# Small products of TensorE regrouped in a decoder block: sums, diagonals, transposes, and the first value weights

## The chip, the core and the metric

The kernel runs on one core of a Trainium2 chip. The metric is the device time of one execution in microseconds (us). Each time is the median of several runs. A profiled execution gives, beside its own time, the span from the first to the last instruction on the core's engines: TensorE (PE, with its weight loads as PEld), VectorE (DVE), ScalarE (ACT), GpSimd (POOL) and SyncE (SP, which issues DMAs).

## What is computed

A decoder block for 256 tokens and a width of 1024, in float32. Cut to what matters:

```
h    = rmsnorm(x);  proj = h @ w_in          # latents 384 + 256, 64 rope columns, q k v (8 x 128), gates
y_a  = attention(rope/latent q, k, v) @ w_o_mla   # q, k, v from rmsnorm(latents) @ w_uq, w_ukv
y_b  = attention(rope(q), rope(k), v) @ w_o_moba  # one block of 256 keys, causal
x    = x + (g_a * y_a + g_b * y_b) @ w_out        # g = sigmoid(gates)
h    = rmsnorm(x)
x    = x + (silu(u1) * u2) @ w_down               # u = causal conv of width 3 over h @ w_up
out  = rmsnorm(x)
```

Both attention branches have 8 heads. Each is causal softmax attention over 256 keys. The norms of the latents need the sum of squares over 384 and over 256 features for each token.

## The kernel before

Activations lie in SBUF with features on partitions and tokens along the row, so that most products have 128 x 128 weights as the stationary operand and 256 tokens as the moving one. For the values and the output projection it is the other way: 128 tokens are stationary and 512 weight columns move. Every product is done in three: both operands are split into a high half, rounded to fp32r, and a low half (the rest), and high x high, low x high and high x low are summed in one PSUM bank (`mm3`, L341). `split` (L346) makes the halves: ScalarE copies with rounding, VectorE subtracts.

Weights arrive in units of 2048 columns (1 MB), one DMA each from SyncE, in a fixed order (`PLAN`, L63). Three buffers hold raw units (`raw`), three the high halves (`whi`), three the low halves (`wlo`). `weights` (L353) issues the load of a unit and splits it in two pieces of 1024 columns.

Order of work: eight input tiles and the latents' weights ("first"), the values (four units "v", two for each half of the columns, `proj_tokens`, L463), then for each of four pairs of heads of the MoBA branch q, gate and k units and one call of `attention` (L603), then four calls for the latent branch, the output projections, and the FFN stage with 22 "up" units.

The order of instructions on each engine is not written by hand. `Program` (L144) records all operations with their dependencies; operations recorded inside `P.together()` form one atom that is issued without a break and that depends on all that its parts need. `emit` (L212) then runs a list scheduler: on each engine it takes, among the operations that are ready at the time at which the engine could go on, the one that was recorded first. Times come from a table of prices (`price`, L283): a transpose 0.11 us, a float32 product 4 x 0.107 us, GpSimd's power 0.63 us and its other operations 0.15 us and a little for each element, and fixed delays between engines. SyncE's loads keep their recorded order. On the chip the engines run in the emitted order and wait on semaphores.

The places that the change touches:

- Rows from columns: a factor for each token (such as the inverse root mean square) exists with tokens on partitions and is needed as a row on all partitions. `to_rows` (L439) multiplies the identity by the factor on VectorE (a diagonal, tile `diag`, two buffers) and multiplies a matrix of ones by it on TensorE in plain float32. It is called for the input's factor (L545), for both latents' factors (L581) and for the FFN's factor (L821).
- The sums of squares of the latents are four float32 products with one column of ones (`lat_sums`, L562). They are recorded between the products of the second half of the values (`between`, L474), after the first four of eight groups.
- From the sums, VectorE and GpSimd form the latents' factors (`r_lat`, L572 to L578): for each latent VectorE multiplies, GpSimd scales, raises to -0.5 and multiplies.
- `keep_values` (L551) scales the values out of PSUM and splits them; for the second half it is recorded before the factors (L571).
- In `attention` the normalised exponentials of a head (tile `e`) are transposed by TensorE, three blocks of 128 x 128, split into `ph` and `pl`, and multiplied with the values into a bank `av`; then the second head follows.

PSUM has eight banks: three `mm`, three `sc`, two `av`, each used in turn.

Of the kernel before, what the change touches and what calls it, by code (L numbers as in the profile page):

```python
# [8 lines left out]


# [2 lines left out]

# [1 line left out]

# [13 lines left out]
S = 256  # L29
# [277 lines left out]
def hybrid_block(ctx: ExitStack, tc: tile.TileContext, x, par, con, fnorm, wpack, out):  # L307
# [3 lines left out]
    P = Program(tc.nc)  # L311
    act, dve, pool, pe, sp = P.act, P.dve, P.pool, P.pe, P.sp

    def T(name, shape, dt=F32):
        return sb.tile([128] + shape, dt, tag=name, name=name)
# [14 lines left out]
    sc_bank = Ring("sc", 3, [512], space=ps)  # L330
    av_bank = Ring("av", 2, [512], space=ps)
# [6 lines left out]
    def mm(o, l, r, start, stop, skip=True):  # L338
        pe.matmul(o, lhsT=l, rhs=r, start=start, stop=stop, skip_group_check=skip)
# [6 lines left out]
    def split(hi, lo, src):  # L346
        act.copy(hi, src)
        dve.tensor_sub(lo, src, f32(hi))
# [1 line left out]

    units = iter(range(len(PLAN)))

    def weights(kind, i, *cuts):  # L353

        u = next(units)
        assert PLAN[u] == (kind, i), (PLAN[u], kind, i)
        n = SIZE.get(kind, UNIT)
        raw, hi, lo = raws(), his(), los()
        cuts = cuts or (n // 2, n)
        sp.dma_start(raw[:, :n], wpack[u, :, :n])  # L360
        a = 0
        for b in cuts:
            split(hi[:, a:b], lo[:, a:b], raw[:, a:b])
            a = b
        return hi, lo

    def groups(wv, k, c):
        return [t.rearrange("p (m k c) -> p m k c", k=k, c=c) for t in wv]
# [3 lines left out]
    ident = cst[:, 4 * S : 4 * S + 128]  # L372
# [8 lines left out]
    ones = T("ones", [128])  # L381
    pool.memset(ones, 1.0)
    o = av_bank()
# [7 lines left out]
    xh, xl = T("XH", [KT, S], F32R), T("XL", [KT, S], F32R)  # L391
# [42 lines left out]
        used[0] += n  # L434
        return smalls[:, used[0] - n : used[0]]

    diag = Ring("diag", 2, [128])

    def to_rows(o, col2):  # L439

        for tt in range(2):
            dg = diag()
            dve.tensor_scalar(dg, ident, col2[:, tt : tt + 1], None, op0=ALU.mult)
            mm(o[:, 128 * tt : 128 * tt + 128], ones, dg, True, True, False)

    def feature_tile(o, m, w, ah, al, ks, first, last):
# [13 lines left out]
                                 m == 0 and k == 0, k > 0)  # L460
        return o

    def proj_tokens(kind, i0, o, ah, al, *between):  # L463

        for part in range(2):
            wv = groups(weights(kind, i0 + part), 4, 512)
            for k4 in range(4):
                k = 4 * part + k4
                with P.together():
                    for tt in range(2):  # L470
                        c = slice(128 * tt, 128 * tt + 128)
                        mm3(o[tt], ah[:, k, c], al[:, k, c], wv[0][:, 0, k4], wv[1][:, 0, k4],
                            k == 0, k == KT - 1)
                if k < len(between):  # L474
                    between[k]()

    def two(ap):
        return ap[:, None, :].to_broadcast([ap.shape[0], 2, S])
# [24 lines left out]
    lat, sq = gate[:, 0:6], gate[:, 6:11]  # L503
# [7 lines left out]
    for j in range(KT // 2):  # L511
        wv = first_unit(j)
        for kk in range(2):
            k = 2 * j + kk
# [25 lines left out]
    rsqrt(r1, ss[:, 0:2], D, 2)  # L540
    pool.tensor_tensor(r1sq, r1, r1, op=ALU.mult)

    rbc, c1, s1 = (T(t, [S]) for t in ("rbc", "c1", "s1"))
    p = sc_bank()
    to_rows(p[:, 0:S], r1)  # L545
    act.copy(rbc, p[:, 0:S])
    dve.tensor_mul(lat[:, 5], lat2[:, S:], rbc)
    dve.tensor_mul(c1, cos1, rbc)
# [2 lines left out]
    def keep_values(o, n):  # L551
        c = slice(512 * n, 512 * n + 512)
        for tt in range(2):
            act.activation(vbh[:, tt, c], o[tt], AF.Copy, scale=r1[:, tt : tt + 1])
            dve.scalar_tensor_tensor(vbl[:, tt, c], o[tt], r1[:, tt : tt + 1],
                                     f32(vbh[:, tt, c]), op0=ALU.mult, op1=ALU.subtract)

    keep_values(v0, 0)

    lat_ss = sc_bank()  # L560

    def lat_sums(j, tt):  # L562

        mm(lat_ss[:, 2 * j + tt : 2 * j + tt + 1], sq[:, 3 * j, 128 * tt : 128 * tt + 128],
           ones[:, 0:1], True, True)

    v1 = [mm_bank(), mm_bank()]
    for j, f in ((0, 1), (0, 2), (3, 4)):
        dve.tensor_add(sq[:, j], sq[:, j], sq[:, f])
    proj_tokens("v", 2, v1, xh, xl, *(partial(lat_sums, j, tt) for j in range(2) for tt in range(2)))  # L570
    keep_values(v1, 1)  # L571
    r_lat = small(4)  # L572
    for j, n in enumerate((QL, KVL)):
        c = slice(2 * j, 2 * j + 2)
# [2 lines left out]
        rsqrt(r_lat[:, c], t, n, 2)  # L577
        pool.tensor_tensor(r_lat[:, c], r_lat[:, c], r1, op=ALU.mult)  # L578
    p = sc_bank()
    for j in range(2):  # L580
        to_rows(p[:, S * j : S * j + S], r_lat[:, 2 * j : 2 * j + 2])  # L581
    lt = T("LT", [2, 5, S], F32R)
    lth, ltl = lt[:, 0], lt[:, 1]
    for f in range(5):
# [12 lines left out]
                                 op0=ALU.mult, op1=ALU.subtract)  # L597


    exps = T("e", [768])  # L600
    phs, pls = (Ring(t, 2, [384], F32R) for t in ("ph", "pl"))

    def attention(i, q, k, more, scale, vh, vl, yh, yl):  # L603


        heads = range(2)

        banks = [sc_bank(), sc_bank()]
        for qt, p in enumerate(banks):
            n = 128 * qt + 128  # L610
            t = slice(128 * qt, n)
            p = p[:, : 2 * n].rearrange("p (a k) -> p a k", a=2)
            with P.together():
                for hh in heads:
                    mm3(p[:, hh], *(a[:, hh, t] for a in q), *(a[:, hh, :n] for a in k), hh == 0,
                        not more)
                if more:
                    mm3(p, *(a[:, t] for a in more[0]), *(a[:, :, :n] for a in more[1]), False,
                        True)
        views = [p[:, :n].rearrange("p (a k) -> p a k", a=2) for p, n in zip(banks, (256, 512))]  # L620
        e = [exps[:, 0:256], exps[:, 256:768]]
        e = [t.rearrange("p (a k) -> p a k", a=2) for t in e]
        mx, nm, sm, rs = (small(4) for _ in range(4))
        for qt in range(2):
            c = slice(2 * qt, 2 * qt + 2)
            diagonal = views[qt][:, :, 128 * qt :]
            dve.tensor_add(diagonal, diagonal, mask[:, None, :].to_broadcast([128, 2, 128]))
            dve.reduce_max(mx[:, c], views[qt], axis=AX.X)
            dve.tensor_scalar(nm[:, c], mx[:, c], -scale, None, op0=ALU.mult)
            for hh in heads:  # L630
                j = 2 * qt + hh
                act.activation(e[qt][:, hh], views[qt][:, hh], AF.Exp, bias=nm[:, j : j + 1],
                               scale=scale, accum_out=sm[:, j : j + 1])
        dve.reciprocal(rs, sm)
        o = av_bank()
        for hh in heads:
            for qt in range(2):
                j = 2 * qt + hh
                act.activation(e[qt][:, hh], e[qt][:, hh], AF.Copy, scale=rs[:, j : j + 1])

            p = sc_bank()
            with P.together():
                for b, t in enumerate((e[0][:, hh], e[1][:, hh, :128], e[1][:, hh, 128:])):
                    pe.transpose(p[:, 128 * b : 128 * b + 128], t, ident)
            ph, pl = phs(), pls()
            split(ph, pl, p[:, :384])
            r = o[:, S * hh : S * hh + S]
            c = slice(128 * (2 * i + hh), 128 * (2 * i + hh) + 128)
            with P.together():
                mm3(r, vh[:, 0, c], vl[:, 0, c], ph[:, :S], pl[:, :S], hh == 0, False)  # L650
                mm3(r[:, 128:], vh[:, 1, c], vl[:, 1, c], ph[:, S:], pl[:, S:], False, True)
        split(yh[:, 2 * i : 2 * i + 2], yl[:, 2 * i : 2 * i + 2], v2(o))
# [155 lines left out]
    def up_unit(i, ph, pl):  # L808

        wv = groups(weights("up", i), KT, 128)  # L810
        o = mm_bank()
        order = [(m, k) for m in range(2) for k in (0, 4)]
        if i == 0:
            order = [(m, k) for k in (0, 4) for m in range(2)]
        for m, k in order:
            with P.together():
                feature_tile(o, m, [t[:, m] for t in wv], x2h, x2l, range(k, k + 4),
                             m == 0 and k == 0, k > 0)
        if i == 0:
            p = sc_bank()  # L820
            to_rows(p[:, 0:S], r2)  # L821
            act.copy(rbc2, p[:, 0:S])
        us, ac = tas(), tbs()

        def w(m, tap):
            c = P_CW + 2 * FT * tap + i + FT * m
            return prm[:, c : c + 1]

        dve.tensor_mul(us, v2(o), two(rbc2))
        for m in range(2):  # L830
            f = i + FT * m
            act.activation(ac[:, m], us[:, m], AF.Identity, scale=w(m, 2),
                           bias=prm[:, P_CB + f : P_CB + f + 1])
            for tap, d in ((1, 1), (0, 2)):
                dve.scalar_tensor_tensor(ac[:, m, d:], us[:, m, : S - d], w(m, tap), ac[:, m, d:],
                                         op0=ALU.mult, op1=ALU.add)
        act.activation(us[:, 0], ac[:, 0], AF.Silu)
        dve.tensor_mul(us[:, 1], us[:, 0], ac[:, 1])
        split(ph, pl, us[:, 1])
# [129 lines left out]
```

## Time and profile before

| | |
|---|---|
| median of three runs | 447.87 us (447.54 to 449.29) |
| profiled execution | 447.01 us |
| its span | 445.2 us |
| TensorE's granted clock in it | 0.997 of full speed |
| busy: PE / PEld / DVE / ACT / POOL | 435.9 / 415.2 / 357.7 / 273.0 / 10.5 us |

Busy times of TensorE overlap, because a product starts before the end of the one ahead; the step from start to start is what a product costs. One float32 product stands as two records in the trace (a transpose as one). A record's line is L246 throughout, where the scheduler calls the engine, so tiles tell the operations apart: `wlo<-raw,whi` is the low half of weights, `sc<-diag,ones` the product with a diagonal, `sc<-ones,gate` a latents' sum, `sc<-cst,e` a transpose of exponentials, `av<-whi,XH` a values product of the first half and `mm<-whi,XH` one of the second.

### The profile page before, as it was taken

The page shows a single profiled execution, that of the slowest core. Times are in us where ns is not written, and L with a number is a line of the kernel's source. Part 1 is how long each engine was busy: PE and PEld are TensorE (multiplying, and loading weights), DVE is VectorE, ACT ScalarE, POOL GpSimd, SP SyncE. Part 2 cuts the span into 40 slices and gives each one's busy share as a digit, 9 for nine tenths or more (in the row PEclk, how much of TensorE's full clock was granted, in tenths as well). Part 3 has the DMA queues.
Part 4 walks back from the last instruction along what each step waited for, and adds up shares of the span by engine and source line. Part 5 has one row for each costly group of instructions (what it writes and reads, how often), then busy time and mean ns, then how long its engine had stood idle before and what let it go on. Part 6 is the DMA issues. An engine that isn't in the chain of part 4 may idle for free.

```text
span 445.2 us, 8253 instructions
## 1 busy us (share of the span) xinstructions
PE 435.9 (98%) x3366; PEld 415.2 (93%) x3366; DVE 357.7 (80%) x553; ACT 273.0 (61%) x471; POOL 10.5 (2%) x25
## 2 busy tenths in 40 slices
PE   8999999999999999999999999999999999999993
PEld 6988999999999999999998899999999999999982
DVE  5669998798879886993788569998787797797765
ACT  5687547455735676788665658765565565565523
POOL 0012000000000000000000010000000000000003
PEclk9999999999999999999999999999999999999998
DMA  7986655435452443240479355386555555556002
GB/s 285 392 337 219 255 188 191 160 125 188 162 181 98 153 173 113 94 191 3 176 301 343 125 190 187 105 299 209 193 205 194 197 198 201 193 200 227 2 0 94
DMA packets 12997, 81.77 MB, mean 184 GB/s; under 512 B 1568, under 2 KB 2208, under 8 KB 4256
## 3 DMA queue, kind: packets, MB, share of 16 engines
q1 hardware_dynamic: 12528, 80.85, 50.4%
q8 instruction: 26, 0.43, 0.4%
q10 hardware_dynamic: 432, 0.40, 0.3%
q14 instruction: 11, 0.09, 0.1%
HBM read 80.20 MB, written 1.05 MB: 182 GB/s over the span
## 4 chain that ended last, share of the span: by engine, by line
PE 89%; DVE 4%; DMA 3%; ACT 1%; issue 1%; POOL 1%; SPq 0%; POOLq 0%; ACTq 0%; DVEq 0%
PE mm L246 63%; PE sc L246 13%; PE av L246 13%; DMA raw<-in_wpack 3%; DVE wlo L246 2%; POOL smalls L246 1%; DVE gate L246 1%; DVE VL L246 1%; ACT whi L246 0%; SPq L246 0%; DVE B L246 0%; ACT tb L246 0%; POOLq L964 0%; DVE tb L246 0%; ACT VH L246 0%
## 5 line engine op out<-in xcount | busy, mean ns | idle before, releaser
L246 DVE TENSOR_TENSOR wlo<-raw,whi 128x1024 fp32r<-128x1024 f32 (+4 forms) x155 | 175.7, 1147 | 36.1 <-ACT whi L246 35.6
L246 ACT CAST whi<-raw 128x1024 fp32r<-128x1024 f32 (+3 forms) x153 | 151.2, 1000 | 85.0 <-PE mm L246 65.7
L246 PE MATMUL mm<-XH,whi 128*128 128x256 f32 x656 | 176.9, 279 | 0.0
L246 PE MATMUL mm<-XL,whi 128*128 128x256 f32 x656 | 175.1, 277 | 0.0
L246 PE MATMUL mm<-XH,wlo 128*128 128x256 f32 x656 | 175.0, 276 | 0.0
L246 PEld LDWEIGHTS mm<-XH,whi 128*128 128x128 f32 x656 | 120.6, 188 | 1.1 <-ACT whi L246 0.6
L246 PEld LDWEIGHTS mm<-XL,whi 128*128 128x128 f32 x656 | 120.6, 188 | 0.4
L246 PEld LDWEIGHTS mm<-XH,wlo 128*128 128x128 f32 x656 | 120.4, 188 | 0.0
L246 DVE SCALAR_TENSOR_TENSOR tb<-ta,prm,tb 128x255 f32<-128x255 f32 x88 | 40.4, 480 | 2.2 <-ACT tb L246 0.7
L246 ACT ACTIVATE tb<-ta,prm 128x256 f32<-128x256 f32 x44 | 24.2, 594 | 3.8 <-DVE ta L246 3.8
L246 PE MATMUL sc<-whi,ql 128*128 128x512 f32 (+1 forms) x66 | 23.4, 355 | 0.0
L246 PE MATMUL sc<-wlo,qh 128*128 128x512 f32 (+1 forms) x66 | 23.3, 353 | 0.0
L246 PE MATMUL sc<-whi,qh 128*128 128x512 f32 (+1 forms) x66 | 23.1, 351 | 0.0
L246 ACT ACTIVATE e<-sc,smalls 128x128 f32<-128x128 f32 (+1 forms) x32 | 13.3, 420 | 12.8 <-DVE smalls L246 11.9
L246 ACT CAST qh<-ta 128x256 fp32r<-128x256 f32 (+1 forms) x26 | 11.3, 435 | 12.4 <-DVE ta L246 12.4
L246 DVE TENSOR_TENSOR ta<-ta,tb 128x256 f32<-128x256 f32 (+1 forms) x35 | 16.9, 484 | 2.2 <-ACT ta L246 0.7
L246 DVE TENSOR_TENSOR ta<-mm,rbc 128x512 f32<-128x512 f32 x22 | 15.2, 689 | 4.2 <-PE mm L246 4.2
L246 PE MATMUL mm<-YBH,whi 128*128 128x256 f32 x64 | 18.1, 283 | 0.0
L246 PE MATMUL mm<-YBH,wlo 128*128 128x256 f32 x64 | 17.7, 277 | 0.0
L246 PE MATMUL mm<-VH,whi 128*128 128x256 f32 x64 | 17.7, 277 | 0.0
L246 PE MATMUL mm<-YBL,whi 128*128 128x256 f32 x64 | 17.7, 277 | 0.0
L246 PE MATMUL mm<-VH,wlo 128*128 128x256 f32 x64 | 17.7, 276 | 0.0
(169 smaller groups left out, 741.8 us busy)
## 6 DMA issues: line engine op xcount, KB each, us to landing
raw<-in_wpack SPq DMA_DIRECT2D x66, 1024.0 KB, 4.8
raw<-in_wpack SPq DMA_DIRECT2D x7, 512.0 KB, 7.2
raw<-in_wpack SPq DMA_DIRECT2D x4, 832.0 KB, 4.2
B<-in_x SPq DMA_DIRECT2D x1, 1024.0 KB, 9.7
gate<-in_x SPq DMA_DIRECT2D x1, 1024.0 KB, 4.8
cst<-in_con SPq DMA_DIRECT2D x1, 641.0 KB, 10.7
raw<-in_wpack SPq DMA_DIRECT2D x2, 256.0 KB, 3.2
gate<-in_fnorm SPq DMA_DIRECT2D x1, 512.0 KB, 5.5
```

The source lines that it names most:

```text
L246: getattr(getattr(self.nc, e), method)(*args, **kw)
```

## The change

- `weights` takes a number of loads. The first unit of the values is loaded in two DMAs of 1024 columns and split in three pieces (512, 512 and 1024 columns).
- `to_rows` is divided into `to_diag`, which makes both diagonals on VectorE, and the products. The diagonals lie in six slots of 128 columns in the tile of the exponentials, which is made earlier; the tile `diag` goes.
- The four sums of the latents are recorded with the two products for the input's factor, ahead of the second half of the values, as one atom. VectorE's three additions that they need are recorded ahead of it.
- The products for both latents' factors are one atom. `keep_values` of the second half is recorded after it.
- In `attention` the six transposes of both heads are one atom, then come both splits, then both products with the values. The `av` bank is taken after the splits.
- The two products for the FFN's factor are one atom.

```diff
-    def weights(kind, i, *cuts):
+    def weights(kind, i, *cuts, loads=1):
...
-        sp.dma_start(raw[:, :n], wpack[u, :, :n])
+        for j in range(loads):
+            c = slice(n * j // loads, n * (j + 1) // loads)
+            sp.dma_start(raw[:, c], wpack[u, :, c])
...
-    diag = Ring("diag", 2, [128])
-
-    def to_rows(o, col2):
-
-        for tt in range(2):
-            dg = diag()
+    exps = T("e", [768])
+    diags = iter(exps[:, 128 * (j % 6) : 128 * (j % 6) + 128] for j in range(8))
+
+    def to_diag(col2):
+        dgs = [next(diags) for _ in range(2)]
+        for tt, dg in enumerate(dgs):
             dve.tensor_scalar(dg, ident, col2[:, tt : tt + 1], None, op0=ALU.mult)
+        return dgs
+
+    def to_rows(o, dgs):
+        for tt, dg in enumerate(dgs):
             mm(o[:, 128 * tt : 128 * tt + 128], ones, dg, True, True, False)
...
-            wv = groups(weights(kind, i0 + part), 4, 512)
+            if (kind, i0, part) == ("v", 0, 0):
+                wv = weights(kind, 0, 512, 1024, 2048, loads=2)
+            else:
+                wv = weights(kind, i0 + part)
+            wv = groups(wv, 4, 512)
...
-                if k < len(between):
-                    between[k]()
...
+    for j, f in ((0, 1), (0, 2), (3, 4)):
+        dve.tensor_add(sq[:, j], sq[:, j], sq[:, f])
     rbc, c1, s1 = (T(t, [S]) for t in ("rbc", "c1", "s1"))
-    p = sc_bank()
-    to_rows(p[:, 0:S], r1)
+    p, lat_ss = sc_bank(), sc_bank()
+    dgs = to_diag(r1)
+    with P.together():
+        for j in range(2):
+            for tt in range(2):
+                mm(lat_ss[:, 2 * j + tt : 2 * j + tt + 1],
+                   sq[:, 3 * j, 128 * tt : 128 * tt + 128], ones[:, 0:1], True, True)
+        to_rows(p[:, 0:S], dgs)
...
-    proj_tokens("v", 2, v1, xh, xl, *(partial(lat_sums, j, tt) for j in range(2) for tt in range(2)))
-    keep_values(v1, 1)
+    proj_tokens("v", 2, v1, xh, xl)
...
-    for j in range(2):
-        to_rows(p[:, S * j : S * j + S], r_lat[:, 2 * j : 2 * j + 2])
+    dgs = [to_diag(r_lat[:, 2 * j : 2 * j + 2]) for j in range(2)]
+    with P.together():
+        for j in range(2):
+            to_rows(p[:, S * j : S * j + S], dgs[j])
+    keep_values(v1, 1)
...
-        o = av_bank()
         for hh in heads:
             for qt in range(2):
                 j = 2 * qt + hh
                 act.activation(e[qt][:, hh], e[qt][:, hh], AF.Copy, scale=rs[:, j : j + 1])
-            p = sc_bank()
-            with P.together():
+        p = [sc_bank() for _ in heads]
+        with P.together():
+            for hh in heads:
                 for b, t in enumerate((e[0][:, hh], e[1][:, hh, :128], e[1][:, hh, 128:])):
-                    pe.transpose(p[:, 128 * b : 128 * b + 128], t, ident)
-            ph, pl = phs(), pls()
-            split(ph, pl, p[:, :384])
+                    pe.transpose(p[hh][:, 128 * b : 128 * b + 128], t, ident)
+        pv = [(phs(), pls()) for _ in heads]
+        for hh in heads:
+            split(*pv[hh], p[hh][:, :384])
+        o = av_bank()
+        for hh in heads:
+            ph, pl = pv[hh]
...
-            to_rows(p[:, 0:S], r2)
+            dgs = to_diag(r2)
+            with P.together():
+                to_rows(p[:, 0:S], dgs)
```

## Rows read from the trace of the kernel before

**Rows 1.** The page's table of engines: busy us, share of the span, instructions.
```profile
PE 435.9 (98%) x3366; PEld 415.2 (93%) x3366; DVE 357.7 (80%) x553; ACT 273.0 (61%) x471; POOL 10.5 (2%) x25
```
**Rows 2.** TensorE's waits in the whole run: total us, times, longest.
```profile
PE av L246 <- DVE warm L246: 1.2, 1, 1.2
PE sc L246 <- DVE diag L246: 0.5, 1, 0.5
PE av L246 <- DVE wlo L246: 0.2, 1, 0.2
```
**Rows 3.** Timeline of TensorE, first values products: start, us, operation, [idle before <- releaser].
```profile
21.59 0.39 PE L246 MATMUL av<-whi,XH 128*128 128x512 f32 x1
22.18 0.50 PE L246 MATMUL av<-wlo,XH 128*128 128x512 f32 x1 [0.20 <-DVE wlo L246]
22.52 0.39 PE L246 MATMUL av<-whi,XL 128*128 128x512 f32 x1
```
**Rows 4.** Timelines of ScalarE and VectorE, the same weights' halves.
```profile
19.82 2.00 ACT L246 CAST whi<-raw 128x1024 fp32r<-128x1024 f32 x2 [3.65 <-DMA raw<-in_wpack]
20.90 1.23 DVE L246 TENSOR_TENSOR wlo<-raw,whi 128x1024 fp32r<-128x1024 f32 x1 [3.74 <-ACT whi L246]
```
**Rows 5.** Timeline of SyncE, the loads of the first two values units.
```profile
12.08 2.88 SPq L246 DMA_DIRECT2D raw<-in_wpack  x2
```
**Rows 6.** Timeline of VectorE, 33 to 52 us.
```profile
35.69 2.35 DVE L246 TENSOR_TENSOR wlo<-raw,whi 128x1024 fp32r<-128x1024 f32 x2
...
41.01 1.21 DVE L246 TENSOR_TENSOR wlo<-raw,whi 128x1024 fp32r<-128x1024 f32 x1
...
47.69 1.40 DVE L246 SCALAR_TENSOR_TENSOR VL<-mm,smalls,VH 128x512 fp32r<-128x512 f32 x2
49.01 0.47 DVE L246 TENSOR_SCALAR diag<-cst,smalls 128x128 f32<-128x128 f32 x2
```
**Rows 7.** Timeline of TensorE, 40 to 52 us.
```profile
40.18 0.39 PE L246 MATMUL mm<-wlo,XH 128*128 128x512 f32 x1
...
45.45 0.61 PE L246 MATMUL sc<-diag,ones 128*128 128x128 f32 x4
...
48.52 0.28 PE L246 MATMUL mm<-XH,wlo 128*128 128x256 f32 x1
49.34 0.71 PE L246 MATMUL sc<-diag,ones 128*128 128x128 f32 x4 [0.54 <-DVE diag L246]
49.81 0.37 PE L246 MATMUL mm<-XH,whi 128*128 128x256 f32 x1
```
**Rows 8.** Timeline of TensorE, first diagonals and one latents' sum.
```profile
33.06 0.61 PE L246 MATMUL sc<-diag,ones 128*128 128x128 f32 x4
...
34.67 0.39 PE L246 MATMUL mm<-whi,XL 128*128 128x512 f32 x1
34.90 0.28 PE L246 MATMUL sc<-ones,gate 128*128 128x1 f32 x2
35.04 0.48 PE L246 MATMUL mm<-whi,XH 128*128 128x512 f32 x1
35.36 0.40 PE L246 MATMUL mm<-wlo,XH 128*128 128x512 f32 x1
```
**Rows 9.** The chain of waits at two attention calls: start, us, what.
```profile
121.46 1.39 PE mm L246 x12
122.85 0.33 PE sc L246 x3
123.18 1.42 PE mm L246 x12
...
146.77 0.66 PE sc L246 x6
147.43 2.74 PE mm L246 x24
```
**Rows 10.** Timeline of GpSimd, the same operation at two places.
```profile
29.03 0.19 POOL L246 TENSOR_SCALAR smalls<-smalls 128x2 f32<-128x2 f32 x1
...
41.11 1.16 POOL L246 TENSOR_SCALAR smalls<-smalls 128x2 f32<-128x2 f32 x1 [10.83 <-DVE smalls L246]
```

More of the change, by code (lines that the diff above doesn't have):

```diff
@@ L11 @@
 from contextlib import ExitStack, contextmanager
-from functools import partial
 import numpy as np
@@ L461, in proj_pair, with proj_tokens @@
         return o
-    def proj_tokens(kind, i0, o, ah, al, *between):
+    def proj_tokens(kind, i0, o, ah, al):
         for part in range(2):
-            wv = groups(weights(kind, i0 + part), 4, 512)
+            if (kind, i0, part) == ("v", 0, 0):
[3 more added lines that the diff above has]
+            wv = groups(wv, 4, 512)
             for k4 in range(4):
@@ L558, in hybrid_block @@
     keep_values(v0, 0)
[L560 to L565, printed above, removed]
     v1 = [mm_bank(), mm_bank()]
-    for j, f in ((0, 1), (0, 2), (3, 4)):
-        dve.tensor_add(sq[:, j], sq[:, j], sq[:, f])
-    proj_tokens("v", 2, v1, xh, xl, *(partial(lat_sums, j, tt) for j in range(2) for tt in range(2)))
-    keep_values(v1, 1)
+    proj_tokens("v", 2, v1, xh, xl)
     r_lat = small(4)
@@ L597, in hybrid_block @@
                                  op0=ALU.mult, op1=ALU.subtract)
-    exps = T("e", [768])
     phs, pls = (Ring(t, 2, [384], F32R) for t in ("ph", "pl"))
```

## The prediction

> **What bounds the kernel now.** I read the page's table of engines first. TensorE is busy 435.9 of 445.2 us, so a microsecond is won only where TensorE waits or where it spends time between useful products [rows 1]. Next the waits of TensorE: after the start two are left, 0.5 us for diagonals from VectorE and 0.2 us for the low halves of the first value weights [rows 2]. The timeline of TensorE then gives the price of each, from start to start of its products, since their ends overlap. Last I read the chain of waits, which is TensorE for most of its length, for what small products cost between large ones. The profiled run took 447.01 us, 1.8 more than its span; the median of the three timed runs is 447.87, so 0.86 above the profiled one. I make the sum against 447.01 and shift the result by 0.86.
>
> **First value weights in two loads and three pieces.** The first values product starts at 21.59, the second, which needs the low halves, at 22.18 and the third at 22.52 [rows 3]. An undisturbed step of this kind is 0.23 (34.67 to 34.90) [rows 8]. So the two steps from 21.59 to 22.52 lose (0.59 - 0.23) + (0.34 - 0.23) = 0.47 us. The cause stands on ScalarE and VectorE: the first 1024 columns are rounded from 19.82, after ScalarE waited 3.65 us for the load, and VectorE starts on their low halves at 20.90 [rows 4]. One product needs 512 columns only. With pieces of 512, half of ScalarE's 1.0 us and of VectorE's 1.23 us goes ahead of the first low halves, so they are there about 1.1 us earlier (21.0 in place of 22.1), before TensorE asks at 21.8, even if the first half of the load lands no earlier than the whole does now. I count 0.47 gained. The second load costs one more issue on SyncE; behind the two issues that begin at 12.08 SyncE spends 2.88 us, most of it waiting for the next buffer, so the issue is hidden there [rows 5]. The last piece is wanted by the third of four products' groups, 2.7 us after the first (12 steps of 0.23), and two further passes of 1.0 and 1.23 us end before that. What is late next is the second unit: its rounding stands behind ScalarE's copies of the latents, which hang on the end of the first stage and do not move. TensorE has no wait there now [rows 2]; if its low halves came just in time, part of the gain would end there, so the bounds are 0 and 0.47.
>
> **Six diagonals.** Now there are two tiles, so the second pair for the latents' factors waits for TensorE to use the first pair and then stands behind the low halves and the values' parts on VectorE: it comes at 49.01 [rows 6]. TensorE's product with it starts at 49.34, the product before at 48.52; a step there is 0.11, so 0.71 us are lost. Its four records are then busy for 0.71 where the same group at 45.45 takes 0.61: 0.10 more [rows 7]. With six tiles both pairs can be made as soon as the factors exist, and the sums that they need are moved ahead of the second half of the values, so they exist several microseconds earlier. The eight records then stand together where the first four stand now, at about 45. I count 0.81 gained; the wait that is shown alone is 0.54. The values' parts now stand behind four diagonals and the products with them. They free a bank by 49.09; the unit that may write it starts after the 24 products from 49.81, that is at 52.5, so some 3 us of cover.
>
> **Latents' sums in one stretch.** Each of the four sums now costs (35.36 - 34.67) - 2 x 0.23 = 0.23 us between products of 512 columns, for two records [rows 8]; together 0.92. In one stretch with the two products with diagonals, what does a record cost? The nearest rows are the transposes, which stand both ways: three take 0.33, six take 0.66 [rows 9], so 0.11 each and nothing for being together. Eight sum records at 0.11 are 0.88: a gain of 0.03, which I take. The other end is a pair at its own step of 0.14 (34.90 to 35.04) with the return to the large products paid once: 4 x 0.14 = 0.56, a gain of 0.36. Below nothing: the factors' row is copied 0.9 us later, as its atom is longer; who waits for it are the tables of the rotation on VectorE, ahead of the low halves of the fourth values unit, which are begun at 35.69 and first used at 40.18 [rows 6, 7]. The first of the two (2.35 for both) ends near 36.9, so about 2.8 us of cover once TensorE comes 0.47 earlier.
>
> **Both heads' transposes side by side.** In four of the eight attention calls (the first three and the seventh; the third stands for them in the rows) the two groups stand apart, in the other four they already stand together. Transposes cost 0.11 either way. What differs are the products around them: apart, 12 products take 1.39 after the first group and 1.42 after the second; together, 24 take 2.74 [rows 9]. That is 2.81 against 2.74: 0.07 for each call, 0.28 for four. Bounds: nothing, and 0.5 if the long stretches of steps above 0.114 that follow a second group go too. The change adds a wait: the first head's transposes wait for the second head's exponentials. On TensorE nothing is held up as long as the planner finds other products, and it has always found them. Nothing is moved past a DMA queue here. The reading of ph and pl comes closer together; their two buffers each suffice for a pair of heads. Joining the last two diagonal products of the FFN stage is worth nothing by the same 0.11.
>
> **Sum.** 0.47 + 0.81 + 0.03 + 0.28 = 1.59 us. 447.01 - 1.59 = 445.4 for a run like the profiled one; 447.87 - 1.59 = 446.3 for the median. Nothing later takes it back, as I see it: behind 50 us TensorE has no wait at all [rows 2].
>
> **Rivals.**
> *The change of kind costs more than I say.* After small products the next large step is 0.32 in place of 0.23 (35.04 to 35.36), 0.09 more [rows 8]. If that is a price for every return, and a joined stretch pays it once, then four sums, one diagonal group, four transposes and the last diagonal pair save ten returns: 0.90 in place of the 0.03 and 0.28 above. Gain 2.18, time 445.7; with the 0.28 of slower products beside it 2.46, 445.4. For it: the 0.09 is there after every group. Against it: three and six transposes cost the same apiece.
> *The waits are only moved.* Every order on every engine is planned anew from prices; VectorE may be late at another place, as it is now at 49.34 although the plan did not mean it. Each such place would cost about what this one does, 0.8 us; two of them leave nothing: 447.9. For it: VectorE's values' parts and diagonals follow one another there without a gap (1.40 from 47.69, then 49.01) [rows 6]. Against it: TensorE shows just two such places in the whole run.
> *Slower: VectorE stands at the diagonals.* GpSimd forms the factors in six small operations. One of them took 0.19 us at 29.03 with VectorE idle, and the same one 1.16 us at 41.11, ending just after VectorE's 1.21 us subtraction that began at 41.01 [rows 6, 10]. The stretch of sums and diagonals begins where the diagonals do now, at 33.06 less 0.47, and lasts 1.3 [rows 8]; so the chain starts near 34.3, ahead of two 1.2 us subtractions and more of that kind. Six operations at 1.16 and some 0.1 between them end near 41.9. If the planner puts the diagonals ahead of the low halves that now start at 35.69, VectorE stands until then, needs 0.9 us for four diagonals (0.47 for two) and 1.2 for the first half: 44.0, where TensorE wants it at 39.7. That is 4.3 lost against 1.6 won: 447.87 + 2.7 = 450.6. It decides from a wait of 2.8 us on. Against it: the code prices the two chains at about 2 us together, so in the plan the diagonals come ready behind these halves.
> The Trainium skill has the rule for this, in "SBUF — State Buffer", section "SBUF: two separate sides": VectorE with two SBUF inputs and GpSimd share a pair of ports under a lock, and the second blocks for the whole instruction of the first. The pair 0.19 and 1.16 agrees with it. By that rule the chain does last to about 42, and the time would be 450.6 if the order on VectorE is the bad one, and the forecast's otherwise.
>
> **Chances.** Forecast (gain 0.9 to 2.2): 0.59. Dearer returns (gain above 2.2): 0.20. Waits moved (gain of -0.5 to 0.9): 0.14. VectorE at the diagonals: 0.07, most of it beyond 450.1. A measurement of this kernel can tell about 0.5% from no change, 2.24 us: faster is below 445.6, slower above 450.1. So faster 0.20, same 0.74, slower 0.06. The range is 445.0 to 447.6. The low end is a gain of 2.7 (0.47 + 0.81 + 0.90 and the 0.5 of the transposes' upper bound), 445.2, and 0.2 for the scatter of a median; the high end is a gain of 0.3, which leaves out the worse part of the moved waits and the slower rival.
>
> **What would show it.** Right: the second values product follows the first after 0.23; one stretch of twelve small records near 32.6 and one of eight near 45, with no wait before it; twelve large products after a joined group in about 1.37; last TensorE product about 1.6 earlier. Wrong: a wait of TensorE on the low halves near 40; a wait on exponentials before a group of six; small records at clearly under 0.11 a step in the long stretches; a gap for VectorE or GpSimd that reaches TensorE.

## The result, and the profile after

The changed kernel took 453.14 us in the median of 16 runs (448.21 to 454.07), the kernel before 447.74 beside it: a ratio of 1.0107, 95% interval 1.0089 to 1.0124. It is slower by 4.8 us (5.4 from the medians), where 446.3, 1.6 less, was forecast. The profiled execution of it is the shortest of the 16 (448.21 us, span 446.4; the other 15 took 451.61 or more), so the run that profiles the same kernel once more (452.76 us, span 450.9) stands beside it below.

TensorE is still busy for nearly all of the span, against [rows 1]:

```profile
PE 436.6 (98%) x3366; PEld 416.1 (93%) x3366; DVE 358.2 (80%) x554; ACT 273.1 (61%) x472; POOL 9.4 (2%) x25
```

TensorE's waits (total us, times, longest), against [rows 2]. Both old ones behind the start, on the diagonals and on the first low halves, are gone; two new ones have come, 0.8 and 0.3 us:

```profile
PE av L245 <- DVE warm L245: 1.2, 1, 1.2
PE mm L245 <- ACT VH L245: 0.8, 1, 0.8
PE mm L245 <- DVE VL L245: 0.3, 1, 0.3
```

TensorE's timeline at the first values products, against [rows 3] (start, us, operation). The steps are 0.23 from the first on, where they were 0.59 and 0.34 in the profile before:

```profile
21.67 0.39 PE L245 MATMUL av<-whi,XH 128*128 128x512 f32 x1
21.90 0.39 PE L245 MATMUL av<-wlo,XH 128*128 128x512 f32 x1
22.13 0.39 PE L245 MATMUL av<-whi,XL 128*128 128x512 f32 x1
```

This is not the change's doing alone. Five runs below (the joined transposes alone, the pair joined alone, the tiles' places alone, the second pair, the six in a row) keep the old load and pieces of these weights. None of their five profiles lists the wait, and all have steps of 0.23 here. One of them, the pair joined alone:

```profile
21.64 0.39 PE L246 MATMUL av<-whi,XH 128*128 128x512 f32 x1
21.87 0.39 PE L246 MATMUL av<-wlo,XH 128*128 128x512 f32 x1
22.10 0.39 PE L246 MATMUL av<-whi,XL 128*128 128x512 f32 x1
```

So the 0.47 us of the profile before is a loss of that execution, and not of every one.

The chain of waits of the first 52 us (start, us, what), against [rows 7, 8]. It is TensorE throughout: twelve small records (1.34) and, eleven us later, eight (0.89), with nothing waited for. 45.16 is the place where four records stood at 45.45; the second group, at 49.34 before, has joined it:

```profile
21.84 10.99 PE av L245 x48
32.82 1.34 PE sc L245 x12
34.16 11.00 PE mm L245 x48
45.16 0.89 PE sc L245 x8
```

The chain around the third attention call and at the start of the latent branch, against [rows 9]. Six transposes stand together (0.66), and the products behind them cost 4.10 / 36 = 0.114:

```profile
121.02 0.66 PE sc L245 x6
121.68 4.10 PE mm L245 x36
...
149.96 6.93 PE mm L245 x36
156.88 2.43 PE sc L245 x18
```

The 36 products that start at 149.96 started at 151.49 before; counted from the first values product (21.67, and 21.59 before) that is 1.61 us gained in the first 150 us, against 1.59 forecast. The agreement is in part luck: 129.90 us is what the one profile before needs for this part, and three other profiles with the same instructions up to there (the pair joined alone, the second pair, the six in a row) need 130.33, 129.44 and 130.32. All of the gain, and more, is lost behind it. The timeline of TensorE at the new waits shows the first loss: the steps from 213.25 and from 214.30 are 1.05 and 0.73, where a step is 0.11, so 1.56 us are lost:

```profile
213.25 0.28 PE L245 MATMUL mm<-VH,wlo 128*128 128x256 f32 x1
214.30 0.38 PE L245 MATMUL mm<-VH,whi 128*128 128x256 f32 x1 [0.77 <-ACT VH L245]
215.03 0.39 PE L245 MATMUL mm<-VL,whi 128*128 128x256 f32 x1 [0.34 <-DVE VL L245]
```

The second loss is no wait. The chain of the run that profiles the changed kernel again shows the group of four small records of the FFN's factor (266.29), and behind it 120 products in 14.14 us and 96 in 11.31, 0.1178 each:

```profile
260.84 5.46 PE mm L245 x48
266.29 0.45 PE sc L245 x4
266.74 14.14 PE mm L245 x120
...
286.41 11.31 PE mm L245 x96
```

The shortest run has the same group, and behind it the same products at 0.1136 (10.91 / 96), as the kernel before has them. Ahead of the group it is the other way round: there its 48 products take 5.66, the slow step, where the other run's take 5.46:

```profile
260.75 5.66 PE mm L245 x48
266.41 0.44 PE sc L245 x4
266.86 13.62 PE mm L245 x120
...
285.96 10.91 PE mm L245 x96
```

The stretch recurs nine times, with the down products between, up to the end of the kernel. From the start of the first down product to the end of the last the shortest run needs 157.9 us, the other 162.1.

### The profile page after: what moved, and what is told of

It is laid out like the page before. It is cut to its first block, busy times and chain, and to the rows that moved or that the text cites. A ratio compares the mean times of both kernels' runs of the same rounds, so it can differ in the third digit from the quotient of the medians.

```text
span 446.4 us, 8260 instructions
## 1 busy us (share of the span) xinstructions
PE 436.6 (98%) x3366; PEld 416.1 (93%) x3366; DVE 358.2 (80%) x554; ACT 273.1 (61%) x472; POOL 9.4 (2%) x25
## 3 DMA queue, kind: packets, MB, share of 16 engines
HBM read 80.20 MB, written 1.05 MB: 182 GB/s over the span
## 4 chain that ended last, share of the span: by engine, by line
PE 94%; ACT 3%; DVE 1%; POOLq 0%; issue 0%; ACTq 0%; DVEq 0%; POOL 0%
PE mm L245 68%; PE sc L245 14%; PE av L245 13%; ACT gate L245 1%; ACT e L245 1%; DVE gate L245 0%; DVE B L245 0%; ACT B L245 0%; ACT L245 0%; ACT tb L245 0%; POOLq L981 0%; ACT ph L245 0%; DVE VL L245 0%; ACT VH L245 0%; ACTq L245 0%
## 5 line engine op out<-in xcount | busy, mean ns | idle before, releaser
L245 ACT CAST whi<-raw 128x1024 fp32r<-128x1024 f32 (+4 forms) x154 | 151.6, 995 | 88.4 <-PE mm L245 67.0
L245 PE MATMUL mm<-VL,whi 128*128 128x256 f32 x64 | 18.1, 282 | 0.3 <-DVE VL L245 0.3
```

Source lines behind the costliest of these rows:

```text
L245: getattr(getattr(self.nc, e), method)(*args, **kw)
```

## The experiments

The kernel before, beside each of them, took between 447.38 and 447.70 us. The first four runs were planned with the profiled run of the changed kernel alone, in which the FFN is quick. Theory A: the latent branch's joined transposes make TensorE wait at 213 us and leave it in a slow step for a stretch. Rival B: the new places of the tiles in SBUF make it slow. Rival C: the 5 us that the profiled run lacks are one more wait somewhere. From the fifth run on, C stands for another theory, that the joined pair for the FFN's factor makes the FFN slow, and D for the places.

**The changed kernel again.** No edit.

> The changed kernel once more, for a second trace. Theory A (late split): the joint transposes of the latent branch make the last attention call late, TensorE waits about 1.5 us at its heads' split near 213 us, and behind that wait the products keep a step of 0.118 in place of 0.113 us, over a stretch that differs from run to run: median 453, and a trace of a run near 453 shows the 0.118 over some 1000 products (5 us) where the first trace shows it over 165. Rival B (placement): the tiles lie elsewhere in SBUF and that slows single operations: then the step is 0.113 and other operations are longer throughout. Rival C: the extra 5 us are a wait at one place that the first trace happened not to have.

Measured: 452.55 us, ratio 1.0115 (1.0093 to 1.0137). It has the wait at 213 us, the step of 0.118 from there to 248 us (the 154 products from 215.94 take 18.14), 0.113 from 248 to 266, and 0.118 to the end. So the slow step ends and begins again, and the long one does not begin at the wait. No further wait is listed, so the first rival C is out.

**The latent branch's calls in their old form.** In `attention`, after the exponentials' sums:

```diff
+        if more is None:
             p = [sc_bank() for _ in heads]
...
+        else:
+            o = av_bank()
+            for hh in heads:
...
```

`more` is None in the first four calls; the other branch is the old form.

> The changed kernel, but the four attention calls of the latent branch take one head after the other as before; the MoBA calls keep the joint transposes. A: no wait at 213 us and no long stretch at 0.118, so the 1.5 us gained in the first 190 us stay: 446.2. B: still above 451, since the tiles lie as in the changed kernel.

Measured: 450.65 us, 1.0073 (1.0056 to 1.0091). The wait at 213 us is gone, and the FFN is slow all the same (96 products in 11.31). A, which expected 446.2, is wrong on the larger part.

**The joined transposes alone.** The kernel before with the changed form of `attention` in all eight calls, and nothing else.

> The kernel before with the joint transposes alone, in all eight calls. A: all of the loss and only 0.3 of the gain, so 453 to 454.5. B: 447.5, since the tiles lie as before.

Measured: 449.89 us, 1.006 (1.0038 to 1.0082). It has the wait at 213 us (0.8 and 0.3), and its FFN goes at 10.91 for 96. So the wait does not bring the slow FFN. The time lies between what A and what B expected. It is 2.2 us above the kernel before; the wait's 1.8 (below) less a few tenths gained in the earlier calls would be about 1.5, and the rest is not explained.

**All but the joined transposes.** The changed kernel with the old `attention` in all calls.

> The changed kernel with the attention of before in all eight calls: first value weights, diagonals and sums alone. A: 447.7 less 1.3, so 446.4; against the run with the old latent calls it says what the MoBA calls' joint transposes are worth (0.3 expected). B: above 451.

Measured: 451.47 us, 1.0092 (1.0071 to 1.0113), with the slow FFN, as B expected. The three kernels with a slow FFN have, beside the parts at the front, two things that the run with the joined transposes alone lacks: the new places of the tiles, and the two products for the FFN's factor joined. In all three the slow step begins right behind that pair. The next four runs set these two apart.

**The pair apart.** The changed kernel with

```diff
             dgs = to_diag(r2)
-            with P.together():
-                to_rows(p[:, 0:S], dgs)
+            to_rows(p[:, 0:S], dgs)
```

> The changed kernel with the two diagonal products of the FFN factor (r2) recorded apart, as in the kernel before; nothing else undone. Theory C (the joined FFN pair): four small records in a row just before the FFN switch TensorE into its slower rhythm (a 256-column product every 0.118 us, not 0.113), which then lasts to the end of the FFN. Apart, the FFN goes at 0.113 and the 4.8 us are back: 452.6 - 4.8 + at most 0.5 = 447.8 to 448.4, the rest above the forecast being the 1.55 us of waiting at 213 us. Theory D (placement in SBUF: the exponentials' tile was moved ahead and the diagonals lie in it): the pair has nothing to do with it, the FFN still goes at 0.118, 452 to 453.

Measured: 447.75 us, 1.0015 (1.0003 to 1.0026). The FFN goes at 10.91, with the front parts and the places as in the changed kernel.

**The pair apart and the latent calls old.** Both edits above.

> The changed kernel with two things undone: the latent branch's four attention calls in their old form, and the r2 products apart. Theory C: no slow rhythm in the FFN and no wait at 213 us, so what the first 190 us gain stays: 450.65 - 4.5 = 446.2 (445.8 to 446.8), my first forecast. Theory D: the FFN still goes at 0.118, 450 to 451.5.

Measured: 445.95 us, 0.9968 (0.9958 to 0.9978), without a wait behind the start. This is faster than both kernels, by 1.48 us of 447.43, close to the 1.59 of the forecast.

**The pair joined, alone.** The kernel before with

```diff
-            to_rows(p[:, 0:S], r2)
+            dgs = [diag() for _ in range(2)]
+            for tt, dg in enumerate(dgs):
+                dve.tensor_scalar(dg, ident, r2[:, tt : tt + 1], None, op0=ALU.mult)
+            with P.together():
+                for tt, dg in enumerate(dgs):
+                    mm(p[:, 128 * tt : 128 * tt + 128], ones, dg, True, True, False)
```

> The kernel before with one edit: the r2 products joined, all else and every tile's place as it was. Theory C: the FFN falls into the step of 0.118 behind the four records at about 264 us, 447.7 + 4.8 = 452.5 (451.5 to 453). Theory D: 447.7, the FFN at 0.113.

Measured: 452.18 us, 1.0109 (1.0093 to 1.0125), as much as the whole change. Its chain of waits shows the group and the slow step behind it:

```profile
265.77 0.45 PE sc L246 x4
266.22 14.14 PE mm L246 x120
...
285.89 11.31 PE mm L246 x96
```

The granted clock is not what differs. In the view by stretches (stretch, us, busy and count of PE, PEld, DVE, ACT, POOL, then the granted clock, DMA share and GB/s) the kernel before shows the first line and this one the second. Both have 1.00, and both have TensorE busy without a gap:

```profile
300.00:310.00 10.00, 10.00 (x85) 9.79 (x84) 7.78 (x12) 5.29 (x8) 0.00 (x0) 1.00 0.58 199
```

```profile
300.00:310.00 10.00, 10.00 (x79) 9.63 (x78) 7.17 (x11) 5.58 (x8) 0.00 (x0) 1.00 0.57 211
```

**The tiles' places alone.** The kernel before with the exponentials' tile laid out early, the diagonals in it, and the ring of diagonals gone:

```diff
-    diag = Ring("diag", 2, [128])
+    exps = T("e", [768])
+    diags = iter(exps[:, 128 * (j % 6) : 128 * (j % 6) + 128] for j in range(8))
...
-            dg = diag()
+            dg = next(diags)
```

> The kernel before with the tiles placed as in the changed one: the exponentials' tile laid out before the attention's tiles, the diagonals in its six places of 128, no ring of diagonals; the instructions are otherwise those of before. Theory C: 447.7, the FFN at 0.113. Theory D: the slow rhythm comes by the placement alone, 450 to 453.

Measured: 447.68 us, 1.0004 (0.9991 to 1.0016). The FFN goes at 10.91. Theory D (and with it B) is out: the joined pair makes the FFN slow, wherever the tiles lie. The edit moves more than places, though: with six slots the planner puts all eight records of the latents' diagonals together (0.89 at 45.02), and a wait of 0.8 us on VectorE comes at 68 us. So of this run only the FFN's step counts here, and not the equal time.

**A second pair.** The kernel before with the pair joined, and in the second up group

```diff
         dve.tensor_mul(us, v2(o), two(rbc2))
+        if i == 1:
+            p = sc_bank()
+            dgs = [diag() for _ in range(2)]
+            for tt, dg in enumerate(dgs):
+                dve.tensor_scalar(dg, ident, us[:, 0, tt : tt + 1], None, op0=ALU.mult)
+            with P.together():
+                for tt, dg in enumerate(dgs):
+                    mm(p[:, 128 * tt : 128 * tt + 128], ones, dg, True, True, False)
```

> The kernel before with the r2 products joined, as in the run with that edit alone (452.18 us), and with a second joined pair of the same size, fed from the second up group's rows and used by nothing (its result is left out of the computation), some 70 products later. Theory T (a group of three or four small records in a row changes TensorE from one rhythm to the other, whichever it is in; two, six or eight leave it): the second pair changes it back, the step is 0.118 only from about 265.6 to 274 us, and the time is 447.4 + 70 x 0.0045 + 0.45 for the pair = 448.2 (447.6 to 448.8). Theory U (any stretch of more than two small records makes TensorE slow): the slow rhythm stays to the end, 452.2 + 0.45 = 452.6 (452 to 453.2).

Measured: 452.06 us, 1.0114 (1.009 to 1.0137). The chain shows the second group at 274.20; the step is 0.118 ahead of it (8.48 / 72), behind it (5.66 / 48) and to the end:

```profile
265.27 0.45 PE sc L246 x4
265.71 8.48 PE mm L246 x72
274.20 0.44 PE sc L246 x4
274.64 5.66 PE mm L246 x48
...
285.83 11.31 PE mm L246 x96
```

This second group of four does not bring the quick step back, so theory T, by which it had to, falls. In the shortest run of the changed kernel a group of four did stand between the slow step and the quick one.

**Six in a row.** The kernel before with the pair joined and a third product behind it:

```diff
+                mm(p[:, 256:384], ones, dgs[1], True, True, False)
```

> The kernel before with the r2 products joined and a third product of 128 columns behind them in the same stretch (its result is used by nothing), so that six small records stand in a row where four made the FFN slow. Theory T: six leave the rhythm as it is, the FFN goes at 0.113, 447.4 + 0.22 = 447.7 (447.0 to 448.2). Theory U: 452.2 + 0.2 = 452.4.

Measured: 447.35 us, 1.0002 (0.9988 to 1.0016). Six records in the same place, and the FFN is quick:

```profile
266.06 0.67 PE sc L246 x6
266.73 13.62 PE mm L246 x120
...
285.83 10.91 PE mm L246 x96
```

So theory U falls too: a longer group leaves the FFN quick. Two and two apart, and six together, leave it quick; four together in this place made it slow in every profile but that of the shortest run, in which the slow step stood ahead of the group.

Nor do four records do so everywhere. In five profiles with the old front parts a group of four stands at 45 us, and the 24 products behind it keep the quick step in all five. The group at 49 us, behind TensorE's wait for the diagonals, is followed by the quick step in three of them (168 products in 19.05 or 19.06) and by the slow one in two, this run and the pair joined alone. The chain of the latter:

```profile
48.90 0.71 PE sc L246 x4
49.61 19.79 PE mm L246 x168
```

**The front parts alone.** The changed kernel with the old `attention` and the pair apart.

> The changed kernel with the old attention in all eight calls and the r2 products apart: what is left of the change is the first value weights' loads, the earlier diagonals and the sums in one stretch. My sum for these was 0.47 + 0.81 + 0.03 = 1.31 us, so 447.4 - 1.3 = 446.1 (445.7 to 446.6), and it stands 0.28 (four times 0.07) above the run that keeps the MoBA calls' joined transposes (445.95). Rival: the joined transposes carry more than their 0.28, since each leaves out two groups of three records and so a stretch at 0.118 (0.35 us behind some of them): then 446.6 to 447.2.

Measured: 446.04 us, 0.997 (0.9959 to 0.9981): 1.34 us gained, 1.31 forecast. The rival is out. The 36 products ahead of the latent branch start 128.54 us behind the first values product here (150.40 less 21.86), 128.29 with the joined MoBA calls kept (150.81 less 22.52, in the run with the pair apart and the latent calls old): 0.25 for these four calls. Only three of the four had their groups apart, so 0.21 was forecast for them; the fourth call of the forecast's 0.28 is the third latent one.

**Which latent call makes the wait.** With the pair apart, the old form in the third latent call alone, and in the last alone:

```diff
-        if more is None:
+        if more is None or i != 2:
```

with `i != 3` in the second of the two.

> The changed kernel with the r2 products apart and only the third latent call's transposes in their old form. With all four joined it took 447.75 us, with none 445.95; between lies the wait at 213 us. Theory W2 (the third call's joined transposes hold two of the three score banks, so the last call's second scores start late, and twelve more of the other products are issued ahead of them and are missing at the end): the wait at 213 us goes or halves, 446.0 to 446.9. Theory W1 (the last call's own joined transposes make both its halves late): the wait stays, 447.6 to 447.9.

> The same with only the last latent call's transposes in their old form. Theory W1: the wait at 213 us goes, 446.0 to 446.4. Theory W2: the wait stays, 447.5 to 447.9.

Measured: 446.36 us (0.9977, 0.9963 to 0.9992) and 448.11 (1.0016, 1.0003 to 1.0028). With the third call old no wait is listed at 213 us; with the last call old 0.6 and 0.3 us are, and the time is a little above what W2 expected. So W2 has the place right. For its mechanism, the score banks, the rows give no sign, though they do not exclude it, since the splits that come late are also what frees these banks. ScalarE and then VectorE with all four calls joined (the run with the pair apart), at the third call's transposes:

```profile
193.52 0.59 ACT L245 COPY B<-mm 128x512 f32<-128x512 f32 x1 [1.19 <-PE mm L245]
194.01 1.06 ACT L245 CAST whi<-raw 128x1024 fp32r<-128x1024 f32 x1
194.95 0.87 ACT L245 CAST ph<-sc 128x384 fp32r<-128x384 f32 x2
```

```profile
195.10 1.23 DVE L245 TENSOR_TENSOR wlo<-raw,whi 128x1024 fp32r<-128x1024 f32 x1 [0.27 <-ACT whi L245]
196.24 1.01 DVE L245 TENSOR_TENSOR pl<-sc,ph 128x384 fp32r<-128x384 f32 x2
```

The same engines with the third call old:

```profile
194.07 0.58 ACT L245 COPY B<-mm 128x512 f32<-128x512 f32 x1 [1.19 <-PE mm L245]
194.56 0.87 ACT L245 CAST ph<-sc 128x384 fp32r<-128x384 f32 x2
```

```profile
195.29 1.01 DVE L245 TENSOR_TENSOR pl<-sc,ph 128x384 fp32r<-128x384 f32 x2
```

Joined, the six transposes are one atom, and neither head's split can be planned before all six are done. ScalarE is free ahead of that, and the plan puts a weights' rounding (1.06) ahead of both splits there and a weights' subtraction (1.23) ahead of them on VectorE. Counted from the first values product (21.59 here, 22.15 with the third call old) the copy begins at the same place, 171.9, and the low halves start at 174.65 and not at 173.14: 1.5 us late. With them go the values' products (36 products stand between them and the transposes, where 24 do with the third call old) and the last call's scores, and the plan orders ScalarE anew. Its timeline in the changed kernel:

```profile
204.17 1.28 ACT L245 ACT_TABLE_LOAD   x1
205.46 0.51 ACT L245 ACTIVATE gate<-gate,prm 128x256 f32<-128x256 f32 x1
205.88 1.48 ACT L245 ACTIVATE e<-e,smalls 128x128 f32<-128x128 f32 x4
...
210.87 2.91 ACT L245 ACTIVATE gate<-gate,prm 128x256 f32<-128x256 f32 x7
213.68 0.57 ACT L245 CAST VH<-av 128x512 fp32r<-128x512 f32 x1
```

A load of ScalarE's function table and a gate go ahead of the last normalising, and seven gates (2.91) ahead of the last split VH, for which TensorE then waits. With the third call old, and in the kernel before, the table load stands behind the normalising, and five gates (2.12) and two (0.91) go directly ahead of that split. That the late splits bring this order about is argued from these rows; no run changed only ScalarE's order.

## Why the prediction was wrong

- *First weights, diagonals, sums* (0.47, 0.81, 0.03): 1.34 measured together against 1.31, and this agreement is in part luck; the three were not run singly. The timelines of TensorE set them apart. The first weights' 0.47 stood in one profile of six and not in the five others, so it was mis-sized: where the wait does not come there is nothing to gain. The sums give 0.04 (first to second group of small records: 32.91 to 45.29 in the run with the joined transposes alone, 32.66 to 45.00 in the changed kernel; the prediction's own 0.92 - 0.88 is 0.04 too, and not 0.03). The diagonals give 0.85 (from there to the first scores, at 68.80 and at 67.66), right in kind and size. The other 0.45 of the 1.34 is open. The group at 49 us, which the change takes away, is followed by the slow step in two profiles of five, at 0.74 for its 168 products, and this may be part of it. Eight sum records and four of diagonals take 1.34, 0.112 a record, so being together is worth nothing there, as taken.
- *Transposes, four calls* (0.28): right in kind and size for the three MoBA calls, 0.25 against 0.21. The fourth, the third latent call, was put down as 0.07 gained and is the one that brings the wait at 213 us: with that call alone in its old form the time goes from 447.75 to 446.36 (the kernel before took 447.43 and 447.57 beside them).
- *"On TensorE nothing is held up as long as the planner finds other products, and it has always found them"*: wrong for the latent branch. I looked at TensorE alone; joining also puts off the splits on ScalarE and VectorE. The price of the joined latent calls is 447.75 - 445.95 = 1.80 us, and it takes the whole gain. This is the rival "the waits are only moved", at 0.14, with one place at more than twice the 0.8 put on it.
- *"Joining the last two diagonal products of the FFN stage is worth nothing by the same 0.11"*: the step that failed most. The group itself costs what I said (0.45 for four records, 0.22 for two). What the sum lacks is what it does to the products behind it: 0.1178 in place of 0.1136 for the rest of the kernel. Alone it costs 452.18 - 447.43 = 4.75. The trace had shown both steps, 1.42 and 1.39 for twelve products; I priced them as 0.07 a call and did not ask what would happen where nothing follows that ends the slow step. That the joined pair brings the slow step is shown by taking it out and by putting it in alone; by what means it does so is open.
- *"Nothing later takes it back"* rested on the waits alone [rows 2], and no wait is listed for the larger loss.
- *The slower rival, VectorE at the diagonals*: did not come. GpSimd's six operations take 3.4 us (38.04 to 41.42), not the 7.5 that the rival put on them. VectorE makes the two pairs at 39.75 and 41.46, with a weights' subtraction of 1.21 us from 40.16 between them, and TensorE wants them at 45.16. GpSimd's last operation of that chain, alike in form to one of 0.19 us at 29.77, ends just behind that subtraction:

```profile
40.73 0.69 POOL L245 TENSOR_TENSOR smalls<-smalls 128x2 f32<-128x2 f32 x1
```

This agrees with the Trainium skill, "SBUF — State Buffer", section "SBUF: two separate sides": one of the two engines is shut out while the other's instruction lasts. What it cost was 0.5 us off the path.
- *Dearer returns*: out. By that rival the four sums alone would have saved four returns of 0.09; they saved 0.04 together.

The terms now add up: -1.6 (front and joined MoBA calls) + 1.8 (joined latent calls) + 4.75 (FFN) = 4.95; measured 4.85 in the second series and 5.40 in the first. The 0.45 between them is not explained. Both profiles of the changed kernel have the slow step behind the wait at 213 us (161 products in 19.23), and that of the run with the pair apart does not (18.54); how many of the executions have it is not known.

## What to carry to other kernels

Where TensorE is busy all the time, read the price of a step in every long stretch, for a change can cost more there than in any wait: two small products moved together cost 4.75 us in the 170 us behind them. Before a loss is counted as a gain, see whether it stands in more than one profile: the first weights' 0.47 did not. After a change to a planned order, look at every engine that the moved group feeds, and not only at the one that runs it. Take a change of several parts apart at once: here two of the parts hid a version that is 0.3% faster than the kernel before.

## What the runs showed of the hardware

TensorE has two steady steps for float32 products of 256 columns at a granted clock of 1.00 and without a wait: 0.1136 and 0.1178 us (10.91 and 11.31 for 96); 48 products of 512 columns took 10.99 and 11.20. A step once taken up can last: in the FFN the slow one held from 266 us to the end. At the start of the FFN a group of four small records was followed by the slow one in five profiles of six, a group of six or of two by the quick one. The number four does not settle it: at 45 us four records left the quick step in five profiles of five, at 49 us in three of five. Nor does the group turn one step into the other each time. In the shortest run of the changed kernel a group of eight (259.88) is followed by the slow step and the four by the quick one; in the run with the second pair the slow step stays. What decides, and why one execution of the changed kernel in sixteen went otherwise, stays open.
